# A hybrid encoder layer on one core: the first job tile by tile, dummy products meanwhile, x one tile further ahead, the last weights in other buffers

## The chip, the cores and the metric

The kernel runs on one core of a Trainium2 chip. The metric is the device time of one execution in microseconds; with several executions the median counts.

## The reference

One layer is applied to a prompt of 2048 tokens and to 8 samples of 16 tokens, with the same weights. A normed input is multiplied by one wide matrix; its columns feed a short convolution, a gated recurrence and a stick-breaking attention, and three gates merge them.

```python
def mixer_layer(x, l, conv_past, S0, past_k, past_v, norm_g, w_in, conv_w, lb, ...):
    h = rms_norm(x, norm_g[l])
    (a_x, a_b, a_c, a_z, g_q, g_f, g_i, g_z,
     s_q, s_k, s_v, s_z, m_a, m_b, m_c) = split_cols(h @ w_in[l])      # 1024 x 9216
    y_conv, conv_new = causal_conv(a_c * a_x, conv_w[l], conv_past)
    o_a = a_b * y_conv * jax.nn.silu(a_z)
    ...                                                                # f = lb + (1-lb) sigmoid(g_f), k = 1 - f
    S_new, o_hg = hgrn_scan(S0, q_hg, log_f, k_in, v_hg)
    o_b = rms_norm(o_hg, hg_norm_g[l]).reshape(B, T, W_HG) * jax.nn.silu(g_z)
    q = rms_norm(s_q, q_norm_g[l]); k = rms_norm(s_k, k_norm_g[l]); v = s_v
    o_sb = sb_prompt(q, k, v)                                          # or, for samples, over 1024 cached keys
    o_c = o_sb.reshape(B, T, W_SB) * jax.nn.silu(s_z)
    m = (jax.nn.sigmoid(m_a) * (o_a @ wb_a) + jax.nn.sigmoid(m_b) * (o_b @ wb_b)
         + jax.nn.sigmoid(m_c) * (o_c @ wb_c))
    return x + m @ w_out[l], conv_new, S_new, k, v
```

## The kernel before

TensorE (PE) does every product in float32 by splitting both operands into a high and a low part and adding three products (high-high, high-low, low-high). `split` makes the parts: ScalarE (ACT) copies to the high part (L174), VectorE (DVE) subtracts it to get the low part (L175). GpSimd (POOL) computes the powers of the norms (`rstd_of`, L211 and L213) and fills masks. All DMAs are issued by SyncE (SP), in one queue.

**Tokens.** There are 17 tiles of 128 tokens: tile 0 holds the samples, the others the prompt. They form three groups, each of two chunks: tiles 0-2 and 3-4, then 5-7 and 8-10, then 11-13 and 14-16. `Prepare` readies a group. For a tile, it loads x into `xt` (L562), squares and sums it on ACT (L569), takes the root on POOL, scales it by the root and by `g_bc`, the norm's gain in all partitions, on DVE (L574), transposes it on PE in two halves of four blocks (L585), and splits each half into `hh` and `hl`. In groups 2 and 3 two tiles are loaded at first, since the pool of `xt` has two buffers, and tile i + 2 is loaded once tile i is transposed. In group 1 all five tiles are loaded at the start, and the first chunk, three tiles, is made ready before the first job.

**Jobs.** For a group, `run_jobs` goes through the columns of `w_in` in jobs. A channel job holds 128 columns still on PE and moves up to 384 tokens of a chunk (`proj_chan`, L660: 24 products for each chunk). A token job (keys `sk`, values `sv`, queries `sq`, recurrence values `gi`) holds the tokens still and moves 256 columns (`proj_tok`, L671: 24 products for each tile). The accumulators (`acc`) are two buffers in this phase. `wload` loads a job's weights in pieces of 512 KB into `wst`, two buffers, and splits them into `w`, three buffers; `wkeep` stores the split weights, 1 MB each, as `W...`, from which later groups load them (L190). Group 1 begins with the gate columns `sz` as a channel job, and the second job is `sk`; job 0 and job 1 run on the first chunk, then both on the second.

**Between and after.** Generators run beside the jobs by a credit of time: the recurrence (`hbg`), attention of the samples during group 2, attention of the prompt from the end of group 2 on (`bg`). `open_attention` opens the pool `at` for the latter; its loads are Q (L260, L261), K (L266) and V (L270). Then follows the merge: for four groups of tiles, jobs multiply the branches by `w_branch` (L1328) and four jobs by `w_out` (L1363), the latter in two weight pieces each. `oh` and `ol` hold the split branch outputs there, two buffers each; a row block `xr` of x is added to an accumulator (L1371) and stored from `yt`. The four output jobs of the last group end the program.

The order in which an engine gets its instructions is set by the framework's scheduler from the order in the program and the buffers; `tc.issue_after(i)` only puts instructions behind `i` on its engine's queue.

## Time and profile before

| | |
|---|---|
| three runs | 2935.62, 2947.18, 2946.2 us; median 2946.2 |
| the profiled execution's own time | 2939.97 us |
| its span | 2938.3 us |
| mean granted clock of TensorE | 0.997 |

In the rows of the profile, times are in microseconds from the span's start unless marked ns. A row of the order of time gives start, length, engine, line, operation, output and inputs with shapes, count, and in brackets how long the engine stood idle before it and who released it. A row of a stretch gives its length and, for PE, weight loads (PEld), DVE, ACT and POOL in turn, busy time and instructions, then the granted clock, the share of DMA and GB/s. `SPq` is SP issuing. A bare piece like `0.44 PE tp L585 x4` comes from the chain of work that ended last, in order of time.

### The profile page before, as it was taken

To read this page: it belongs to the slowest core of one execution; us is meant where nothing else is said; L and a number is where in the kernel's file an instruction comes from. 1 tells how busy PE (TensorE), PEld (TensorE's weight loads), DVE (VectorE), ACT (ScalarE), POOL (GpSimd) and SP (SyncE) were. 2 spreads that over 40 slices of the span, in tenths; PEclk is the share of its full clock that TensorE was granted. 3 is DMA by queue.
4 is the path that set the end of the run, shared out by engine and by line. 5 is a ranking of instruction groups with operands and counts; after the bars stand their busy time and mean duration, and the time that the engine had idled before them with its cause. 6 is when DMAs were issued, how large, how long until landed. Compare 5 with 4: busy or idle time off the path is not lost.

```text
span 2938.3 us, 51261 instructions
## 1 busy us (share of the span) xinstructions
PE 2877.3 (98%) x19467; PEld 2672.8 (91%) x19467; DVE 1533.2 (52%) x3182; ACT 1024.5 (35%) x2359; POOL 429.4 (15%) x859
## 2 busy tenths in 40 slices
PE   8999999999999999999999999999999999999998
PEld 7999999989999999999999999999988787687888
DVE  5345635641342423345434748265677876767743
ACT  4332222242222222114333344334444554444420
POOL 3100000120100000003231111101013412313110
PEclk9999999999999999999999999999999999999999
DMA  8887776767556564535764443434347776677666
GB/s 280 302 272 237 229 229 231 233 224 244 183 192 198 175 211 146 177 128 170 243 193 156 139 153 129 163 116 153 125 148 265 253 263 215 224 234 232 233 229 211
DMA packets 329223, 597.80 MB, mean 203 GB/s; under 512 B 29097, under 2 KB 231170, under 8 KB 291090
## 3 DMA queue, kind: packets, MB, share of 16 engines
q1 hardware_dynamic: 328978, 594.54, 61.5%
q8 instruction: 154, 2.52, 0.4%
q14 instruction: 91, 0.75, 0.1%
HBM read 410.62 MB, written 183.80 MB: 202 GB/s over the span
## 4 chain that ended last, share of the span: by engine, by line
PE 87%; DMA 4%; DVE 3%; issue 3%; POOL 1%; ACT 1%; SPq 0%; DVEq 0%; POOLq 0%; ACTq 0%
PE acc L660 44%; PE acc L671 13%; PE acc L1363 6%; PE acc L1328 5%; PE pv L334 4%; PE tp L289 3%; PE z L985 2%; PE z L305 2%; PE z L304 2%; DMA w<-W 2%; DVE pr L317 1%; PE tp L432 1%; POOL mp L1337 1%; PE pv L496 1%; DMA ost<-OX 1%
## 5 line engine op out<-in xcount | busy, mean ns | idle before, releaser
L660 PE MATMUL acc<-hh,w 128*128 128x384 f32 (+1 forms) x5376 | 1466.5, 338 | 1.3 <-ACT w L174 0.8
L660 PEld LDWEIGHTS acc<-hh,w 128*128 128x128 f32 x5376 | 965.6, 188 | 25.6 <-issue 17.9
L660 PE MATMUL acc<-hl,w 128*128 128x384 f32 (+1 forms) x2688 | 883.3, 329 | 0.0
L660 PEld LDWEIGHTS acc<-hl,w 128*128 128x128 f32 x2688 | 507.9, 189 | 4.9 <-issue 1.0
L671 PE MATMUL acc<-w,hh 128*128 128x256 f32 x2176 | 411.6, 285 | 0.7 <-DVE gm L1078 0.4
L671 PEld LDWEIGHTS acc<-w,hh 128*128 128x128 f32 x2176 | 341.6, 188 | 2.7 <-DVE gm L1078 0.7
L317 DVE TENSOR_TENSOR_SCAN pr<-snb,carry 128x513 f32<-128x513 f32 x192 | 250.8, 1307 | 118.3 <-ACT snb L308 116.8
L671 PE MATMUL acc<-w,hl 128*128 128x256 f32 x1088 | 306.4, 282 | 0.0
L1328 PE MATMUL acc<-oh,w 128*128 128x512 f32 (+2 forms) x960 | 296.6, 370 | 4.0 <-ACT oh L174 2.5
L290 ACT COPY aT<-tp 128x512 f32<-128x512 f32 (+2 forms) x320 | 167.4, 524 | 290.9 <-PE tp L289 290.6
L322 DVE TENSOR_TENSOR sp<-sp,pr 128x512 f32<-128x512 f32 (+2 forms) x320 | 210.2, 657 | 34.7 <-POOL sp L313 10.0
L1363 PE MATMUL acc<-w,mh 128*128 128x256 f32 x1088 | 212.8, 285 | 7.6 <-DMA w<-W 7.5
L308 ACT ACTIVATE snb<-z 128x512 f32<-128x512 f32 (+2 forms) x320 | 172.3, 539 | 127.9 <-PE z L305 117.2
L1328 PEld LDWEIGHTS acc<-oh,w 128*128 128x128 f32 x960 | 177.5, 191 | 36.4 <-DVE gate L1336 4.4
L671 PEld LDWEIGHTS acc<-w,hl 128*128 128x128 f32 x1088 | 205.2, 189 | 0.4
L317 DVE TENSOR_TENSOR_SCAN pr<-snb,one 128x129 f32<-128x129 f32 (+3 forms) x128 | 115.7, 904 | 160.1 <-POOL snb L313 159.8
L1363 PEld LDWEIGHTS acc<-w,mh 128*128 128x128 f32 x1088 | 173.6, 188 | 17.1 <-issue 6.7
L175 DVE TENSOR_TENSOR w<-wst,w 128x1024 fp32r<-128x1024 f32 x92 | 114.9, 1249 | 137.1 <-ACT w L174 134.7
L289 PE MATMUL tp<-idf,sp 128*128 128x128 f32 x1088 | 172.8, 274 | 8.3 <-ACT aT L290 7.7
L1328 PE MATMUL acc<-ol,w 128*128 128x512 f32 (+1 forms) x480 | 174.7, 364 | 2.7 <-DVE ol L175 2.6
L310 ACT ACTIVATE sp<-z 128x512 f32<-128x512 f32 (+2 forms) x320 | 171.4, 536 | 11.9 <-DMA OX<-ot 6.7
L289 PEld LDWEIGHTS tp<-idf,sp 128*128 128x128 f32 x1088 | 132.0, 141 | 27.3 <-ACT aT L290 10.1
(290 smaller groups left out, 3620.5 us busy)
## 6 DMA issues: line engine op xcount, KB each, us to landing
w<-W SPq DMA_DIRECT2D x204, 1024.0 KB, 5.4
W<-w SPq DMA_DIRECT2D x92, 1024.0 KB, 5.0
wst<-in_w_in_dram SPq DMA_DIRECT2D x72, 512.0 KB, 5.5
GM<-gm SPq DMA_DIRECT2D x120, 192.0 KB, 2.8
Kt<-KT SPq DMA_DIRECT2D x160, 128.0 KB, 3.6
gate<-GM SPq DMA_DIRECT2D x72, 256.0 KB, 3.0
vc<-in_cache_v_dram SPq DMA_DIRECT2D x64, 256.0 KB, 3.2
kc<-in_cache_k_dram SPq DMA_DIRECT2D x64, 256.0 KB, 2.9
```

Source lines behind the costliest of these rows:

```text
L175: return first, (eng or nc.vector).tensor_tensor(lo, src, hi.bitcast(F32), ALU.subtract)
L289: nc.tensor.transpose(tp[:, j * P:(j + 1) * P], sp[:, j * P:(j + 1) * P], idf)
L290: nc.scalar.copy(aT[:, e, 0:nb, i * P:(i + 1) * P], tp[:, :w].rearrange("p (b q) -> p b q", q=P))
L308: nc.scalar.activation(sn[:, 512 - w:512], z[:, :w], AF.Sigmoid, scale=-0.125)
L310: nc.scalar.activation(sp[:, :w], z[:, :w], AF.Sigmoid, scale=0.125)
L317: nc.vector.tensor_tensor_scan(pr[:, 512 - w:513][:, ::-1], s_in, s_in, one if diag else carry[e][i], ALU.mult, ALU.bypass)
L322: nc.vector.tensor_tensor(sp[:, :w], sp[:, :w], pr[:, 513 - w:513], ALU.mult)
L334: nc.tensor.matmul(pv[64 * e:64 * e + 64, c0:n], Vt[:, j, e], aT[:, e, j, c0:n], start=first and j == 0, stop=last and j == nb - 1, skip_g ...
L660: nc.tensor.matmul(acc[:, :n], w[0][a][:, k], hT[b][:, k, :n], start=k == 0 and i == 0, stop=k == KB - 1 and i == 2)
L671: nc.tensor.matmul(acc[:, :256], hT[b][:, k, ti * P:(ti + 1) * P], w[k // 4][a][:, k % 4], start=k == 0 and i == 0, stop=k == KB - 1 and i ...
L1328: nc.tensor.matmul(acc[:, :n], w[0][a][:, k, dd * P:(dd + 1) * P], box[x][b][:, k, sl], start=k == 0 and i == 0, stop=k == 3 and i == 2)
L1363: nc.tensor.matmul(acc[:, :256], box["l" if b else "h"][:, k, ti * P:(ti + 1) * P], w[k // 4][a][:, k % 4], start=k == 0 and i == 0, stop= ...
```

## The change

1. Group 1 starts with the first job on V (`sv`, columns 0 to 255), and this job runs on both chunks before the next. It asks for one tile at a time (`Prepare.tile`), so a tile's square, scaling and transposes stand between the products of the tile before. x of tile 0 and `g_bc` are loaded first, then the job's two weight pieces, then the other four tiles.
2. `keep_busy` puts products of the identity with itself on PE, whose result nobody reads: 14 at the start, four behind each half of tile 0's transposes.
3. The vectors, masks, fills and `rev` are built behind the first job's preparation instead of ahead of or beside it.
4. A third buffer for x (pool `xq`): groups 2 and 3 load three tiles at first and tile i + 3 once tile i is transposed (in group 3 the last tiles go to the two old buffers). The pool is closed before attention's opens, and the first chunk of group 3 is made ready ahead of that.
5. The weights of the last group's second and fourth output job go into buffers of `oh` and `ol`.

```diff
-    first_split = []
-    def wload(pieces, key):
+    def wload(pieces, key, places=None):
...
-            w = wp.tile([P, 2, 1024], F32R, tag="w", name="w")
+            w = places[n] if places else wp.tile([P, 2, 1024], F32R, tag="w", name="w")
...
                 st = wp.tile([P, a, b], F32, tag="wst", name="wst", bufs=2)
                 nc.sync.dma_start(st, v)
-                pair = split(hi, lo, st)
-                if not first_split:
-                    first_split.extend(pair)
+                with ExitStack() as order:
+                    if len(kept) < 1 and n:
+                        for x in prep.last:
+                            order.enter_context(tc.issue_after(x.ins))
+                    split(hi, lo, st)
...
+    p01 = ExitStack()
+    xq = p01.enter_context(tc.tile_pool(name="xq", bufs=1, side="right"))
...
+    def keep_busy(n):
+        z = ps_z()
+        for _ in range(n):
+            nc.tensor.matmul(z[:, 0:P], idf, idf, start=True, stop=True)
+    keep_busy(14)
...
+            self.final = g == len(GROUPS) - 1
...
         def load(self, i):
-            self.fetch(i, xp.tile([P, D], F32, tag="xt", name="xt"))
+            self.fetch(i, self.room(i))
             self.square(i)
+        def room(self, i):
+            return (xq.tile([P, D], F32, tag="xt3", name="xt3") if i == 2 or i % 3 == 2 and not self.final else
+                    xp.tile([P, D], F32, tag="xt", name="xt"))
...
-                for i in range(min(2, n)):
+                for i in range(min(3, n)):
...
-                if i + 2 < n:
-                    self.load(i + 2)
-                    yield
-                if i + 1 >= 2 and i + 1 < n:
-                    self.scale(i + 1)
+                for k in [i + 2] if self.final and i == 3 else [] if self.final and i == 2 else [i + 3]:
+                    if k < n:
+                        self.load(k)
+                        yield
+                if i + 2 >= 3 and i + 2 < n:
+                    self.scale(i + 2)
                     yield
                 self.ready = i
...
-            for i in range(n):
-                self.fetch(i, xp.tile([P, D], F32, tag="xt", name="xt") if i < 2 else
-                           g0p.tile([P, D], F32, tag="xt0", name="xt0", bufs=3))
-                if i == 0:
-                    nc.sync.dma_start(g_bc, norm_g[0].partition_broadcast(P))
-            for f in (self.square, self.scale):
-                for i in range(2):
-                    f(i)
             self.scaled = True
             for i in range(n):
-                if i > 2:
-                    with tc.issue_after(first_split[0].ins), tc.issue_after(first_split[1].ins):
-                        self.square(i)
-                        yield
-                        self.scale(i)
-                        yield
+                if not i:
+                    self.fetch(i, self.room(i))
+                    nc.sync.dma_start(g_bc, norm_g[0].partition_broadcast(P))
+                with ExitStack() as order:
+                    if i:
+                        for x in self.last:
+                            order.enter_context(tc.issue_after(x.ins))
+                    for k in ((0,), (1, 2), (3,), (4,), ())[i]:
+                        self.square(k)
+                    yield
+                    self.scale(i)
+                yield
                 for kk in range(0, KB, 4):
                     self.turn(i, kk)
+                    if not i:
+                        keep_busy(4)
                     yield
-                    if i == 0 and not kk:
-                        self.square(2)
-                if i == 0:
-                    with tc.issue_after(self.last[1].ins):
-                        self.scale(2)
                 self.ready = i
-                yield
+                if not i:
+                    yield
+                    for k in range(1, n):
+                        self.fetch(k, self.room(k) if k < 3 else g0p.tile([P, D], F32, tag="xt0", name="xt0", bufs=2))
...
+            return self.hT[ci]
+        def tile(self, ci, ti):
+            i = self.tiles.index((ci, ti, self.group[ci][ti]))
+            while self.ready < i:
+                next(self.gen)
             return self.hT[ci]
...
-    prep.chunk(0)
+    prep.tile(0, 0)
...
+    def build_vectors():
+        nc.sync.dma_start(qg_bc, q_norm_g[0].partition_broadcast(P))
+        nc.sync.dma_start(kg_bc, k_norm_g[0].partition_broadcast(P))
+        vrow = g0p.tile([17, P], F32, tag="mtmp", name="vrow", bufs=2)
+        nc.sync.dma_start(vrow[0:12], conv_w[0].rearrange("j (b p) -> (j b) p", p=P))
+        nc.sync.dma_start(vrow[12:16], hg_lb_logits[0].rearrange("(h p) -> h p", p=P))
+        nc.sync.dma_start(vrow[16:17], hg_norm_g)
+        pvec = ps_tp()
+        nc.tensor.transpose(pvec[:, 0:17], vrow, idf[0:17, 0:17])
+        nc.vector.tensor_copy(vec, pvec[:, 0:17])
...
+                    acc = yield from proj_tok(w, hT(ti) if callable(hT) else hT, ti)
         filler = [sz_job(j) for j in range(4)] + [gate_job(x, d) for x in range(3) for d in range(8)]
+        if not g:
+            jobs.append(qkv.pop(2))
...
-        order = ([(0, 0), (1, 0), (0, 1), (1, 1)] + order
+        begin = [(0, 0), (1, 0), (0, 1), (1, 1)] if g else [(0, 0), (0, 1), (1, 0), (1, 1)]
+        order = (begin + order
                  + [(n - 2, 0), (n - 1, 0), (n - 2, 1), (n - 1, 1)])
         for at_, (i, ci) in enumerate(order):
             weights(i)
-            weights(i + 1)
-            if not g and at_ == 1:
-                with tc.issue_after(rstd_at[0].ins), tc.issue_after(first_split[1].ins):
+            if g or at_:
+                weights(i + 1)
+            if not g and at_ == 0:
+                prep.advance()
+            if not g and at_ == 2:
+                with tc.issue_after(rstd_at[0].ins), tc.issue_after(prep.last[1].ins):
+                    build_vectors()
+                    build_hist()
+                    build_rev()
                     build_bound()
                     build_masks()
                     build_selectors()
-            hT = prep.chunk(ci)
+            hT = prep.chunk(ci) if g or at_ > 1 else lambda ti, ci=ci: prep.tile(ci, ti)
...
-                if nxt and (left <= 2 or nxt.ready < 0 and len(nxt.xt) < 2 or left <= 3 and not nxt.scaled):
+                if nxt and (left <= 2 or nxt.ready < 0 and len(nxt.xt) < 3 or left <= 3 and not nxt.scaled):
...
+            prep.chunk(0)
             bg.drain()
+            p01.close()
             open_attention()
...
-            ws[i + 1] = wload(*alljobs[i + 1][0])
+            places = None
+            if i + 1 - len(alljobs) in (-3, -1):
+                places = [p3.tile([P, 4, GMAX], F32R, tag=t, name="wlast", bufs=2).rearrange("p a b -> p (a b)")
+                          [:, :2048].rearrange("p (v w) -> p v w", v=2) for t in ("oh", "ol")]
+            ws[i + 1] = wload(*alljobs[i + 1][0], places)
```

`build_hist` (the fills of `uhist`, `shist`, `cstage` and the load of the cached convolution rows) and `build_rev` hold lines that stood at the top level before, as `build_vectors` does. What the scheduler makes of this stands below, engine by engine, at the places where instructions move.

PE, the first instructions; before, x of three tiles is transposed, then the first channel job starts (`vrow` holds the vectors):

```order
L585 MATMUL tp<-idf,xt 128x128 x16
L585 MATMUL tp<-idf,xt_117 128x128 x8
L704 MATMUL tp<-idf,vrow 128x17
L660 MATMUL acc<-hh,w 128x384
L660 MATMUL acc<-hl,w 128x384
L660 MATMUL acc<-hh,w 128x384 x2
```

and now (L553 is `keep_busy`, L602 the transposes, L694 the token job):

```order
L553 MATMUL z<-idf 128x128 x14
L602 MATMUL tp<-idf,xt 128x128 x4
L553 MATMUL z<-idf 128x128 x4
L602 MATMUL tp<-idf,xt 128x128 x4
L553 MATMUL z<-idf 128x128 x4
L694 MATMUL acc<-w,hh 128x256
L694 MATMUL acc<-w,hl 128x256
```

The products of tile 0 follow its own transposes, with 22 dummies around those.

DVE, behind its first five instructions; before:

```order
L574 SCALAR_TENSOR_TENSOR xt<-xt,rr,g_bc 128x1024 x2
L175 TENSOR_TENSOR hl<-tp,hh 128x4x128 x2
L574 SCALAR_TENSOR_TENSOR xt_117<-xt_117,rr,g_bc 128x1024
L175 TENSOR_TENSOR hl<-tp,hh 128x4x128 x4
L706 COPY vec<-tp 128x17
L175 TENSOR_TENSOR w<-wst,w 128x1024
```

and now:

```order
L591 SCALAR_TENSOR_TENSOR xt<-xt,rr,g_bc 128x1024
L175 TENSOR_TENSOR w<-wst,w 128x1024
L175 TENSOR_TENSOR hl<-tp,hh 128x4x128 x2
L175 TENSOR_TENSOR w<-wst,w 128x1024
L591 SCALAR_TENSOR_TENSOR xt<-xt,rr,g_bc 128x1024
L175 TENSOR_TENSOR hl<-tp,hh 128x4x128 x2
```

The remainders of the two weight pieces now stand between the first tile's steps, and a tile's scaling stands behind the low parts of the tile before; the masks, the vectors and the bound follow after the fifth tile, ahead of the first gate product.

SP, the first loads for the prompt's attention; before, at the end of the samples' attention (L528 is its last store):

```order
L528 DMA OX<-oct 128x4x128
L889 DMA OX<-y 128x384
L260 DMA Q_15008<-QT 64x512
L261 DMA Q_15009<-QT 64x512
L190 DMA w<-W_5548 128x2048
```

and now, at the end of group 2 (L579 loads x, L262 and L263 Q, L268 K, L272 V):

```order
L579 DMA xt<-in_x_prompt_dram 128x1024
L1092 DMA OX<-ob 128x256
L1147 DMA GM<-gm 128x384
L262 DMA Q_15038<-QT 64x512
L263 DMA Q_15039<-QT 64x512
L579 DMA xt<-in_x_prompt_dram 128x1024
L262 DMA Q_15038<-QT 64x512
L263 DMA Q_15039<-QT 64x512
L268 DMA Kt<-KT 64x512 x2
L272 DMA Vt<-VV 128x4x128
```

The first heads' Q, K and V moved behind the late loads of group 3's x, one of which stands among them.

SP, the weights of the last jobs, before (L1320 loads a gate, L1358 `xr`; the last two pairs are W_27241, W_27243 and W_27586, W_27588):

```order
L190 DMA w<-W_26519 128x2048
L1320 DMA gate<-GM 128x512 x2
L190 DMA w<-W_26521 128x2048
L1320 DMA gate<-GM 128x512
L190 DMA w<-W_26872 128x2048
L1372 DMA out_dram<-yt 128x256
```

and now (`wlast` is a buffer of `oh` or `ol`; the pairs' numbers are 29 higher):

```order
L189 DMA w<-W_26548 128x2048
L1360 DMA gate<-GM 128x512
L189 DMA w<-W_26550 128x2048
L1360 DMA gate<-GM 128x512 x2
L189 DMA wlast<-W_26901 128x2048
L189 DMA w<-W_27270 128x2048
L189 DMA wlast<-W_27615 128x2048
L1412 DMA out_dram<-yt 128x256 x2
```

The second pair, of which W_26903 went out earlier still, and the first pieces of the third and fourth are now ahead of the first store of the last output rows.

More of the change, by code (lines that the diff above doesn't have):

```diff
@@ L689, in trunk @@
     prep = Prepare(0)
-    prep.chunk(0)
+    prep.tile(0, 0)
     qg_bc = const.tile([P, 64], F32, name="qg_bc")
-    nc.sync.dma_start(qg_bc, q_norm_g[0].partition_broadcast(P))
     kg_bc = const.tile([P, 64], F32, name="kg_bc")
-    nc.sync.dma_start(kg_bc, k_norm_g[0].partition_broadcast(P))
-    vrow = g0p.tile([17, P], F32, tag="mtmp", name="vrow", bufs=2)
-    nc.sync.dma_start(vrow[0:12], conv_w[0].rearrange("j (b p) -> (j b) p", p=P))
-    nc.sync.dma_start(vrow[12:16], hg_lb_logits[0].rearrange("(h p) -> h p", p=P))
-    nc.sync.dma_start(vrow[16:17], hg_norm_g)
-    pvec = ps_tp()
-    nc.tensor.transpose(pvec[:, 0:17], vrow, idf[0:17, 0:17])
-    vec = const.tile([P, 17], F32, name="vec")
-    nc.vector.tensor_copy(vec, pvec[:, 0:17])
+    vec = const.tile([P, 17], F32, name="vec")
+    def build_vectors():
[8 more added lines that the diff above has]
+        nc.vector.tensor_copy(vec, pvec[:, 0:17])
     def tap(j, b):
@@ L1087, in compute @@
                 for ti, t in enumerate(chunks[ci]):
-                    acc = yield from proj_tok(w, hT, ti)
+                    acc = yield from proj_tok(w, hT(ti) if callable(hT) else hT, ti)
                     post(acc, t, s)
```

16 lines of the change are left out of this document (9 added, 7 removed).

## The prediction

> **What bounds the kernel now.** I read the page's first part, then the busy time in stretches chosen around PE's idle time, then the order of time in the stretches that the change touches.
>
> ```profile
> span 2938.3 us, 51261 instructions
> ...
> PE 2877.3 (98%) x19467; PEld 2672.8 (91%) x19467; DVE 1533.2 (52%) x3182; ACT 1024.5 (35%) x2359; POOL 429.4 (15%) x859
> ...
> 0.00:32.24 32.24, 19.72 (x91) 17.61 (x92) 18.45 (x39) 17.03 (x26) 15.12 (x62) 1.00 0.81 270
> ...
> 570.00:612.00 42.00, 37.34 (x259) 34.25 (x257) 23.91 (x59) 16.63 (x41) 7.09 (x14) 1.00 0.77 261
> ...
> 1340.00:1365.00 25.00, 20.69 (x128) 18.95 (x127) 18.39 (x28) 14.20 (x34) 9.15 (x18) 1.00 0.64 216
> ...
> 2196.00:2880.00 684.00, 655.88 (x3910) 539.99 (x3910) 481.55 (x612) 301.31 (x589) 172.81 (x265) 0.99 0.72 238
> 2880.00:2938.30 58.30, 50.39 (x398) 48.30 (x396) 13.45 (x26) 2.30 (x4) 0.00 (x0) 1.00 0.60 202
> ```
>
> TensorE (PE) is busy 2877.3 of 2938.3 us, so every saving is PE idle time or PE time at a low clock. The second number of a stretch row is PE's busy time. Idle: 12.5 us in the first stretch, 4.7 and 4.3 where one token group follows another, 28.1 in the merge stage, 7.9 at the end: 57.5 of all 61.0. The change works on all of these but the merge stage; in the order of instructions nothing is changed from 1365 us to the last output jobs, so the 28.1 us stay.
>
> The start is worse than its 12.5 idle us, as PE also runs slowly there:
>
> ```profile
> 1.18 0.29 POOL masks.py:199 TENSOR_SCALAR_AFFINE_SELECT idf<-idf 128x128 f32<-128x128 f32 x1
> 4.62 1.06 ACT L569 ACTIVATE junk<-xt 128x1024 bf16<-128x1024 f32 x1 [2.55 <-DMA xt<-in_x_sample_dram]
> 6.98 1.29 DVE L574 SCALAR_TENSOR_TENSOR xt<-xt,rr,g_bc 128x1024 f32<-128x1024 f32 x1 [5.24 <-POOL rr L213]
> 7.83 1.06 ACT L569 ACTIVATE junk<-xt 128x1024 bf16<-128x1024 f32 x1 [2.06 <-DMA xt<-in_x_prompt_dram]
> 8.32 1.97 PE L585 MATMUL tp<-idf,xt 128*128 128x128 f32 x8 [8.32 <-DVE xt L574]
> 9.80 0.57 POOL L213 TENSOR_TENSOR rr<-rv,mhalf 128x1 f32<-128x1 f32 x1
> 13.50 0.59 ACT L174 CAST hh<-tp 128x512 fp32r<-128x512 f32 x1 [2.28 <-PE tp L585]
> 14.12 0.69 DVE L175 TENSOR_TENSOR hl<-tp,hh 128x512 fp32r<-128x512 f32 x1
> 17.36 1.05 ACT L174 CAST w<-wst 128x1024 fp32r<-128x1024 f32 x1
> 18.44 1.23 DVE L175 TENSOR_TENSOR w<-wst,w 128x1024 fp32r<-128x1024 f32 x1 [0.17 <-ACT w L174]
> 18.46 0.69 PE L660 MATMUL acc<-hh,w 128*128 128x384 f32 x1 [0.78 <-ACT w L174]
> ...
> 21.80 0.84 PE L660 MATMUL acc<-hh,w 128*128 128x384 f32 x2
> ...
> 24.64 0.59 PE L660 MATMUL acc<-hh,w 128*128 128x384 f32 x1
> ...
> 28.67 0.44 PE tp L585 x4
> ...
> 97.93 7.07 PE acc L660 x48
> 105.00 14.24 PE acc L671 x120
> ```
>
> The last three rows are pieces of the chain: warm, a transpose takes 0.11 us (0.44/4), a 256-column product 0.119 (14.24/120), and a 384-column one 0.178 (7.07 for 24 of each). Cold, eight transposes took 1.97 us, 0.246 each. The first projection starts at 18.46 and the pace stays cold to 24.64. Up to 32.24 us PE did 40 transposes and 48 products of 384 columns, the work of 4.4 + 8.5 = 12.9 warm us: 19.3 us are lost there.
>
> **The start.** The first job is now V's projection (24 products of 256 columns per tile), taken tile by tile as x arrives, its two weight pieces second and third in the queue after g_bc; 14 dummy products stand in front, four more behind each half of the first tile's transposes. Up to the first x tile the chain is the old one: x lands at 4.6, is scaled from 6.98, transposes at 8.32. The dummies can start at 1.5, when the identity is written. An f32 product with 128 columns shows as two records:
>
> ```profile
> 594.52 0.39 PE L1030 MATMUL hg<-vg,sc 128*128 128x128 f32 x2
> 594.74 0.40 PE L1032 MATMUL hg<-Sn,Qd 128*128 128x128 f32 x2
> ...
> 2337.61 0.66 PE L289 MATMUL tp<-idf,sp 128*128 128x128 f32 x4 [2.11 <-ACT aT L290]
> ...
> 2702.35 1.12 PE L289 MATMUL tp<-idf,sp 128*128 128x128 f32 x4 [3.28 <-ACT aT L290]
> ```
>
> The first two rows start 0.22 us apart, so a warm dummy costs 0.22, a cold one 0.49 by the transposes' ratio. Fourteen cold ones take 6.9 us and end at 8.4. PE worked 6.2 us, from 18.46 to 24.64, until it was warm; from 1.5 that is 7.7, so 25 cold records and 3 warm ones end at 8.0. PE stays warm until 8.32: a gap of 2.11 us before 2337.61 left it warm (four transposes in 0.66), while one of 3.28 before 2702.35 did not (1.12). [...]
>
> First tile: transposes 8.32, two batches of four dummies of 0.88 each between and behind, PE free at 11.1. The landings: x0 was there at 4.6 and x1, two DMAs on, at 7.8, so 1.6 us each; a 512 KB weight piece takes 1.95 at the first stretch's mean of 270 GB/s. So w0, where x1 stood, lands near 8.2, w1 near 10.1, x1 near 11.7. ACT: w0's copy (1.05) from 8.2, both halves of hh (0.59) to 10.9, w1's copy to 11.95, then x1's square (1.06 and its read). DVE: w0's remainder (1.23) to 10.5, two hl (0.69) to 11.9, w1's remainder to 13.2. First product at 11.2, tile done at 14.4. x1's square ends at 13.2, POOL's two steps take 0.9, scaling 1.28 from 14.15; transposes at 15.45, product at 17.35. From then a tile needs on DVE and its partners 1.28 + 0.55 (four transposes and latency) + 0.59 + 2 x 0.69 + 0.1 = 3.9 us, on PE 2.85 + 0.88 = 3.73. Three more tiles at 3.9, the last late by about 0.6 for the next weights' remainder on DVE: the job ends at 17.35 + 3 x 3.9 + 0.6 + 2.85 = 32.5. PE has then done 120 products and 40 transposes, 18.7 warm us; before it had 13.2 at that time (12.9 at 32.24 and 0.26 on). **Gain 5.5 us.** Bounds: 7.0 if PE sets the period from the second tile; 2.0 if weights land at half x's pace and the dummies stay cold. The 22 dummies cost nothing else: PE has nothing to do there.
>
> The constants (masks, bound, vectors) moved behind this job stand in DVE's queue ahead of the first gate product, whose accumulator the third accumulator after it needs.
>
> ```profile
> 23.18 0.29 POOL L740 MEMSET mtmp<- 128x128 f32 x2
> ...
> 30.97 0.32 POOL L745 TENSOR_SCALAR_AFFINE_SELECT mtmp<-mtmp 128x1 f32<-128x1 f32 x2
> ```
>
> Before, POOL's masks took 8.1 us between these rows, other fills among them. Now DVE is free for the first at 30.5, by the schedule above; 8.1 us more put the gate product at 38.6, and PE needs the buffer at 32.5 + 7.1 = 39.6. Hidden by 1 us; slower masks would cost what they exceed that by. Stores of V wait on SP for ACT's copies with weight loads behind them, needed 14 us later: nothing.
>
> **x three tiles ahead.** In both later groups the third tile now has a buffer of its own, so each late load comes one tile sooner.
>
> ```profile
> 593.59 1.09 PE L585 MATMUL tp<-idf,xt 128*128 128x128 f32 x8 [0.89 <-DVE xt L574]
> ...
> 605.18 0.65 PE L585 MATMUL tp<-idf,xt 128*128 128x128 f32 x4 [0.49 <-DVE hl L175]
> ...
> 1343.38 0.44 PE L1058 MATMUL tp<-idf,on 128*128 128x128 f32 x2 [0.97 <-DVE hl L175]
> ...
> 1355.98 0.66 PE L585 MATMUL tp<-idf,xt 128*128 128x128 f32 x4 [1.70 <-DVE hl L175]
> ...
> 1362.08 1.06 PE L585 MATMUL tp<-idf,xt 128*128 128x128 f32 x8 [1.15 <-DVE xt L574]
> ```
>
> Waits on x or on what follows it: 0.89 + 0.49 = 1.4 us in the first transition, 0.97 + 1.70 + 1.15 = 3.8 in the second. A tile sooner is about 6 us there (the last two tiles' transposes stand at 1355.98 and 1362.08), more than each wait. But recurrence and attention steps are re-sorted there, and what comes late next is DVE. I take **1.0** (0 to 1.4, and a loss of 1 if the recurrence waits instead) and **2.8** (0 to 3.8). Against the second stands that attention's Q and K loads no longer come early (first rival).
>
> **Last weights.** Output jobs two and four of the last group load into the free oh/ol buffers, so no load waits for the running job.
>
> ```profile
> 2885.76 0.36 PE L1363 MATMUL acc<-w,mh 128*128 128x256 f32 x1 [0.69 <-DMA w<-W]
> ...
> 2899.98 0.39 PE L1363 MATMUL acc<-w,mh 128*128 128x256 f32 x1 [0.28 <-DMA w<-W]
> ...
> 2913.32 0.39 PE L1363 MATMUL acc<-w,mh 128*128 128x256 f32 x1 [1.44 <-DMA w<-W]
> ...
> 2927.04 0.38 PE L1363 MATMUL acc<-w,mh 128*128 128x256 f32 x1 [1.94 <-DMA w<-W]
> ```
>
> The waits are 0.69 + 0.28 + 1.44 + 1.94 = 4.35 us. The last three go (3.66); of the first, whose load now comes one gate load sooner, I take half: **4.0**. Bytes are the same. Next late are xr and y stores, but three accumulators at 2.85 us per tile cover them.
>
> **Sum:** 5.5 + 1.0 + 2.8 + 4.0 = 13.3 off an execution of 2939.97 us (span 2938.3): 2926.7. That execution lies 6.2 below the median of the three runs, 2946.2; against the median, 2946.2 - 13.3 = 2932.9, say 2933, 0.45% less. About 0.5% (14.7 us, 2931.5) is what a measurement of this kernel can tell from no change.
>
> **Rivals.**
> (1) Slower: the new pool must close before attention's pool opens, so the first Q, K, V loads, issued near 1190 us before, now come after the third tile's transposes, with an x load among them that waits for a buffer:
>
> ```profile
> 1190.47 0.52 SPq L260 DMA_DIRECT2D Q<-QT  x1
> ...
> Kt<-KT SPq DMA_DIRECT2D x160, 128.0 KB, 3.6
> ```
>
> Two heads' loads are 13 issues of 0.5 us and a landing of 3.6, with the wait for the x buffer 12.8 us. In the new order PE has 19 transposes and some 41 products, 9.4 us, before the first score, which needs only the first half (8.9). If all 12.8 were uncovered and PE cold after (2.6 more), 15.4 is lost and the 2.8 too: 2946.2 - 10.5 + 15.4 = 2951. It decides once more than 10.5 is uncovered; the cover of 9.4 speaks against.
> (2) The front pays less: the dummies do not release the clock and hold the transposes (8.32 to 14.3 for both batches, about 2.5 us), and each tile takes 4.4 on DVE (1.5 more). Start 1.5: 2937.
> (3) All waits vanish and PE sets the first job's period: 7.0 + 1.4 + 3.8 + 4.35 = 16.6: 2929.6.
> (4) The x loads change nothing, since DVE was the wait: 2946.2 - 9.5 = 2936.7.
>
> **Chances.** Forecast 0.50, (1) 0.04, (2) 0.15, (3) 0.25, (4) 0.06. The runs shown spread from 2935.62 to 2947.18, so the forecast's own range is 2927 to 2938, of which a third is beyond 0.5%: faster 0.25 x 0.85 + 0.5 x 0.36 = 0.39; slower 0.02, part of (1); within 0.59. Range 2922 to 2943: the bounds summed are gains of 16.6 and 4.6 (2.0 - 1 + 0 + 3.6), 2929.6 and 2941.6; the runs' spread adds to both sides, more to the fast one, where the shown times reach 10.6 below their median.
>
> **What would show it.** Dummies from 1.5 to about 8; the first tile's transposes warm; L694 from about 11.4; first job done near 32.5, then no PE gap before 60; PE idle in the first 32 us near 9 with the dummies counted as busy; waits on x gone at both transitions; no wait for w at the end. Wrong if the first products start after 14, if a PE wait for Q or K stands at the second transition, or if the gate product holds PE near 39.

## The result, and the profile after

| | before | after |
|---|---|---|
| first comparison, median | 2946.2 us (5 runs, 2935.62 to 2947.2) | 2922.81 us (5 runs, 2919.97 to 2925.84) |
| ratio, 95% interval | | 0.9932 [0.9919, 0.9945] |
| second and third comparison, ratio | | 0.9949 [0.9936, 0.9962], 0.9942 [0.9930, 0.9954] |
| all executions, median | 2938.95 us (78 runs) | 2922.94 us (15 runs) |
| profiled execution: span, own time, clock | 2938.3, 2939.97, 0.997 | 2918.1, 2919.97, 0.999 |

The change is faster, by 23.4 us in the first medians, by 20.2 us between the two profiled spans, and by 16.0 us between the medians of all executions. The forecast was 13.3 us: 2933 against the first median, 2926.7 against the profiled execution; the range of 2922 to 2943 held the time at its fast end. The three shown times of before had a high median: 78 executions give one 7.3 us lower. So of the 10.1 us by which 2933 was too slow, 7.3 are the median that it started from.

The profile after, first its totals, then the busy time of the first stretch (its granted clock reads 1.00, as before's did, since the column holds 1.00 until the first recorded change, at 25.01 us in before and 4.43 in after; the cold start shows only in the paces of the rows below):

```profile
span 2918.1 us, 51343 instructions
...
PE 2873.3 (98%) x19511; PEld 2672.2 (92%) x19511; DVE 1530.7 (52%) x3182; ACT 1024.7 (35%) x2359; POOL 427.9 (15%) x859
```

```profile
0.00:32.24 32.24, 27.14 (x202) 25.27 (x203) 17.00 (x26) 17.28 (x29) 12.60 (x36) 1.00 0.90 315
```

PE's idle time is 44.8 us instead of 61.0, in the first 32.24 us 5.1 instead of 12.5. The start in order of time:

```profile
1.46 4.80 PE L553 MATMUL z<-idf 128*128 128x128 f32 x28 [1.46 <-POOL idf masks.py:199]
8.17 0.66 PE L602 MATMUL tp<-idf,xt 128*128 128x128 f32 x4 [1.91 <-DVE xt L591]
8.66 1.06 PE L553 MATMUL z<-idf 128*128 128x128 f32 x8
9.55 0.60 PE L602 MATMUL tp<-idf,xt 128*128 128x128 f32 x4
9.99 1.06 PE L553 MATMUL z<-idf 128*128 128x128 f32 x8
10.80 0.36 PE L694 MATMUL acc<-w,hh 128*128 128x256 f32 x1
...
15.16 1.07 PE L602 MATMUL tp<-idf,xt 128*128 128x128 f32 x8 [0.67 <-DVE xt L591]
...
39.02 0.55 DVE L1106 TENSOR_TENSOR gm<-acc,gm 128x384 f32<-128x384 f32 x1
```

The dummies warm PE (28 records in 4.80 us, 0.21 us apart at first and 0.11 from 4.4 us on), the transposes run warm (four in 0.66 us), the first product starts at 10.80 and the second tile's transposes at 15.16. Up to 32.24 us PE did 40 transposes, 117 products of 256 columns and one of 384, or 4.4 + 13.9 + 0.2 = 18.5 warm us: 13.7 are lost instead of 19.3. The first gate product on DVE (L1106) starts at 39.02 and PE waits for nothing there. The transitions, PE's rows with a wait of 0.3 us or more:

```profile
589.15 0.44 PE L1086 MATMUL tp<-idf,on 128*128 128x128 f32 x2 [1.82 <-DVE hl L175]
599.09 0.66 PE L434 MATMUL tp<-idf,kc 128*128 128x128 f32 x4 [0.63 <-DVE hl L175]
616.81 0.39 PE L694 MATMUL acc<-w,hh 128*128 128x256 f32 x1 [1.19 <-DMA w<-W]
...
1334.21 0.44 PE L1086 MATMUL tp<-idf,on 128*128 128x128 f32 x2 [0.97 <-DVE hl L175]
1342.25 0.63 PE L602 MATMUL tp<-idf,xt 128*128 128x128 f32 x4 [0.40 <-DVE xt L591]
1348.22 0.52 PE L602 MATMUL tp<-idf,xt 128*128 128x128 f32 x3 [1.38 <-DVE xt L591]
1351.90 0.33 PE L291 MATMUL tp<-idf,sp 128*128 128x128 f32 x1 [0.46 <-DVE hl L175]
```

In the first, no transpose of x waits any more; in the second, the waits are 0.97, 0.40, 1.38 and 0.46 where they were 0.97, 1.70 and 1.15. The last piece of PE in the chain that ended last:

```profile
2870.90 44.04 PE acc L1403 x366
```

There is no wait for weights in the output jobs. Set against the same instructions of the profiled execution of before, the 20.2 us come from: the start 5.7, the first transition 3.0, the second 0.9, the merge stage (before: 2193 to 2844 us) 5.0, the end behind it 5.2, all else 0.4. (Where the start ends, one channel job of 7.07 us stands on the other side of the recurrence's steps; it is taken out here.)

### The profile page after: what moved, and what is told of

Read it like the earlier page. It is cut to its first block, busy times and chain, and to the rows that moved or that the text cites. A ratio compares the mean times of both kernels' runs of the same rounds, so it can differ in the third digit from the quotient of the medians.

```text
span 2918.1 us, 51343 instructions
## 1 busy us (share of the span) xinstructions
PE 2873.3 (98%) x19511; PEld 2672.2 (92%) x19511; DVE 1530.7 (52%) x3182; ACT 1024.7 (35%) x2359; POOL 427.9 (15%) x859
## 4 chain that ended last, share of the span: by engine, by line
PE 87%; DVE 4%; DMA 4%; issue 3%; POOL 2%; ACT 1%; SPq 0%; DVEq 0%; POOLq 0%; ACTq 0%
PE acc L683 45%; PE acc L694 13%; PE acc L1403 6%; PE acc L1368 4%; PE pv L336 4%; PE tp L291 3%; PE z L1013 2%; PE z L307 2%; PE z L306 2%; DVE pr L319 1%; PE tp L434 1%; POOL mp L1377 1%; DMA w<-W 1%; PE pv L498 1%; DMA gate<-GM 1%
## 5 line engine op out<-in xcount | busy, mean ns | idle before, releaser
L694 PE MATMUL acc<-w,hh 128*128 128x256 f32 x2176 | 413.1, 286 | 1.5 <-DMA w<-W 1.2
L694 PEld LDWEIGHTS acc<-w,hh 128*128 128x128 f32 x2176 | 341.8, 188 | 4.0 <-DMA w<-W 1.5
L694 PE MATMUL acc<-w,hl 128*128 128x256 f32 x1088 | 306.8, 282 | 0.7 <-DVE hl L175 0.7
L694 PEld LDWEIGHTS acc<-w,hl 128*128 128x128 f32 x1088 | 205.1, 189 | 1.8 <-DVE hl L175 1.3
L1403 PE MATMUL acc<-w,mh 128*128 128x256 f32 x960 | 189.1, 285 | 2.5 <-DMA w<-W 2.3
L1403 PEld LDWEIGHTS acc<-w,mh 128*128 128x128 f32 x960 | 153.7, 188 | 10.6 <-issue 5.2
L1146 ACT ACTIVATE gm<-acc 128x384 f32<-128x384 f32 (+1 forms) x144 | 68.3, 474 | 260.8 <-PE acc L683 223.0
```

The lines of the kernel that those rows point to most:

```text
L694: nc.tensor.matmul(acc[:, :256], hT[b][:, k, ti * P:(ti + 1) * P], w[k // 4][a][:, k % 4], start=k == 0 and i == 0, stop=k == KB - 1 and i ...
L1403: nc.tensor.matmul(acc[:, :256], box["l" if b else "h"][:, k, ti * P:(ti + 1) * P], w[k // 4][a][:, k % 4], start=k == 0 and i == 0, stop= ...
```

## The experiments

"Start", "transition", "merge" and "end" are differences to the profiled execution of before, between the same instructions, in us; positive is faster.

| run | kernel | ratio to before, 95% interval | start | 1st transition | 2nd | merge | end |
|---|---|---|---|---|---|---|---|
| e1 | before again | 1.0005 [0.9995, 1.0015] | -2.3 | 0.0 | 0.8 | -2.7 | 1.2 |
| e2 | start alone | 0.9979 [0.9970, 0.9989] | 5.5 | -2.6 | 1.0 | 1.8 | 1.5 |
| e3 | x alone | 0.9989 [0.9978, 0.9999] | -0.8 | 1.8 | 0.6 | -3.6 | 1.6 |
| e4 | last weights alone | 0.9984 [0.9975, 0.9993] | 0.6 | 0.3 | 0.8 | 2.5 | 1.8 |
| e5 | after again | 0.9949 [0.9936, 0.9962] | 5.8 | 2.1 | 0.5 | 1.9 | 4.3 |
| e6 | after, x two ahead | 0.9957 [0.9945, 0.9968] | 5.8 | -1.3 | 0.5 | 2.3 | 4.0 |
| e7 | after, no dummies | 0.9963 [0.9949, 0.9976] | 3.7 | 3.9 | 1.2 | 4.4 | 4.7 |
| e8 | after, 7 dummies at first | none: one execution, 2929.2 us | 3.2 | 2.4 | -0.6 | 0.8 | 4.5 |
| e9 | after, last weights in order | 0.9952 [0.9939, 0.9964] | 5.5 | 3.4 | 0.0 | 3.0 | 6.0 |
| e10 | e9, no dummies | 0.9970 [0.9960, 0.9980] | 3.1 | 4.3 | 0.3 | -1.1 | 6.2 |
| e11 | after, third time | 0.9942 [0.9930, 0.9954] | 5.6 | 4.5 | 0.2 | 5.0 | 4.1 |

The places that a run's kernel leaves as they were (all of e1's) show what executions of one program differ by: up to 2 or 3 us in a place.

**e1, the kernel before again** (no edit).

> The kernel before, unchanged, to get a second trace and the clock beside each time. From 1365 us to the last jobs both traces hold the same instructions, yet the changed kernel was 4.8 us shorter there (2193 to 2878 us before). Theory A: this is not the change's, but the number of cold spells of TensorE after its long waits, which differs from execution to execution; then the runs here spread over 6 us or more, the longer ones have the lower mean clock (0.995 against 0.998), and the stage's idle time stays within 1.5 us of 28.1. Theory B: the stage is shorter because of the change (other times of its loads); then this trace is within 1 us of the first there, and the spread does not go with the clock.

Its profiled execution took 2943.66 us, with PE at a mean clock of 0.996, and it lost 2.7 us in the merge stage against the first. (A cold spell is a time in which PE is granted half its clock, in before for one 0.50 from 2291.46 to 2294.87 us.) Stretches of 20 us of the merge stage with a clock under 1.00, first of before, then of before again, then of after:

```profile
2280.00:2300.00 20.00, 16.40 (x93) 13.86 (x92) 18.75 (x20) 10.45 (x19) 8.20 (x9) 0.91 0.86 275
2300.00:2320.00 20.00, 19.91 (x110) 16.68 (x111) 18.28 (x26) 9.88 (x20) 10.60 (x8) 0.91 0.66 227
2560.00:2580.00 20.00, 18.95 (x106) 13.90 (x107) 13.18 (x18) 8.49 (x17) 0.00 (x0) 0.91 0.72 230
2700.00:2720.00 20.00, 17.65 (x75) 12.66 (x76) 12.04 (x18) 8.45 (x20) 9.71 (x17) 0.83 0.69 222
```

```profile
2200.00:2220.00 20.00, 17.89 (x93) 13.27 (x92) 14.76 (x20) 11.50 (x21) 0.00 (x0) 0.91 0.61 199
2280.00:2300.00 20.00, 16.87 (x99) 14.45 (x96) 17.40 (x19) 9.17 (x16) 8.67 (x9) 0.91 0.78 257
2300.00:2320.00 20.00, 18.22 (x106) 15.82 (x106) 19.29 (x27) 10.53 (x21) 8.37 (x9) 0.91 0.68 235
2340.00:2360.00 20.00, 17.89 (x93) 13.45 (x92) 14.90 (x24) 10.41 (x25) 9.05 (x17) 0.91 0.77 259
2560.00:2580.00 20.00, 17.72 (x104) 12.42 (x103) 11.38 (x17) 8.20 (x16) 0.00 (x0) 0.91 0.67 209
2700.00:2720.00 20.00, 16.96 (x80) 11.95 (x79) 12.19 (x18) 8.19 (x19) 9.81 (x16) 0.91 0.71 210
2760.00:2780.00 20.00, 17.61 (x93) 12.99 (x92) 14.39 (x18) 5.91 (x11) 1.26 (x7) 0.91 0.74 260
```

```profile
2280.00:2300.00 20.00, 18.44 (x109) 16.89 (x110) 19.66 (x24) 11.15 (x21) 8.45 (x9) 0.91 0.76 250
2680.00:2700.00 20.00, 16.75 (x78) 11.64 (x77) 13.13 (x18) 7.09 (x16) 10.16 (x16) 0.91 0.74 233
```

A clock of 0.91 over 20 us is 1.8 us less, or 3.6 at half the clock. Summed over stretches of 10 us, the clock lost in the merge stage was, in all 13 traces, a whole number of times 1.7 us (3.4 at half):

| trace | times 1.7 us | stage's length | its idle time |
|---|---|---|---|
| after | 2 | 646.0 | 27.0 |
| e11 | 3 | 646.1 | 26.2 |
| e2, e4, e5, e7 | 4 | 649.2, 648.5, 649.2, 646.7 | 28.0, 25.8, 27.1, 25.7 |
| before, e8, e9, e10 | 5 | 651.0, 650.2, 648.0, 652.1 | 28.1, 27.0, 25.2, 28.6 |
| e6 | 6 | 648.7 | 25.8 |
| e1, e3 | 7 | 653.7, 654.6 | 27.8, 28.9 |

The length goes with the clock lost, 0.94 us for each (correlation 0.84), while the idle time hardly changes. Over the 73 executions of before whose clock is known, the mean time falls from 2945.6 us at a clock of 0.994 (3 runs) to 2939.0 at 0.997 (34) and 2934.6 at 0.999 (4). What theory A named is there: the 5.0 us that the merge stage gave between the two profiled executions are three cold spells fewer, and executions of one program differ by as many (before again lost 2.7 there with two more; the changed kernel has 2, 4 and 3 in after, e5 and e11). Whether the change makes the spells a little rarer isn't settled: the four traces with all of its parts have 2, 3, 4 and 5, those without any 5 and 7, and the mean granted clock is 0.9976 over the 15 executions of the changed kernel and 0.9970 over the 73, which would be 1.8 us (an estimate, 0.0006 of 2940).

**e2 to e4, each part alone.** Start alone is the changed kernel without the lines on `xq`, on three tiles and on `wlast`; x alone and last weights alone are the kernel before with these lines:

```diff
# x alone
+    xq = p01.enter_context(tc.tile_pool(name="xq", bufs=1, side="right"))
-            self.fetch(i, xp.tile([P, D], F32, tag="xt", name="xt"))
+            self.fetch(i, self.room(i))
-                for i in range(min(2, n)):
+                for i in range(min(3, n)):
...
# last weights alone
+            if i + 1 - len(alljobs) in (-3, -1):
+                places = [p3.tile(...) for t in ("oh", "ol")]
```

> Of the change only the start: the first job on V tile by tile, the dummies, the later constants; x two tiles ahead as before, the last weights in their old buffers. Theory A (the parts add up, each at its own place): 19.3 us lost to the first job's end fall to 13.7, a gain of 5.7 us (ratio 0.998), both transitions and the tail as before: waits on x near 1.4 and 3.8 us, four waits for w of 4.35 at the end. Theory B (the start shifts later loads and thus shortens the merge stage): 10 us or more, ratio 0.9965.

> Of the change only the third buffer for x in groups 2 and 3. Theory A: TensorE idles 2.5 us less in the first transition (570 to 612 us) and about 1 less in the second, of which a late weight load behind the first gives back 0.9: a gain of 2.7 us, ratio 0.999. Theory B (the x loads bring the merge stage's 4.8 too, since attention's first loads moved): 7.5 us, ratio 0.9975. Theory C (the waits there are DVE's, so the loads change nothing): 0.5 us or less.

> Of the change only the buffers of the second and fourth output job's weights. Theory A: the last 55 us become 5.2 us shorter (4.4 idle, 0.8 of restarts), no wait for w there, all else as before: ratio 0.9982. Theory B (the merge stage's 4.8 come from these buffers too, through the order of the loads): 10 us, ratio 0.9966. If only the waits themselves go, without restarts: 4.35.

The ratios are 0.9979, 0.9989 and 0.9984: theory A in all three, 6.2 + 3.2 + 4.7 = 14.1 us. (x alone has an interval of 0.3 to 6.5 us.) The traces add two things. Start alone: 19.3 us lost became 13.7, but the first transition became 2.6 us longer, which theory A did not expect:

```profile
597.48 1.06 ACT L583 ACTIVATE junk<-xt 128x1024 bf16<-128x1024 f32 x1 [1.99 <-DMA xt<-in_x_prompt_dram]
```

```profile
590.61 0.63 PE L599 MATMUL tp<-idf,xt 128*128 128x128 f32 x4 [1.96 <-DVE xt L588]
607.29 1.26 PE L599 MATMUL tp<-idf,xt 128*128 128x128 f32 x8 [1.92 <-DVE xt L588]
```

```profile
580.00:600.00 20.00, 17.76 (x121) 16.96 (x120) 8.29 (x13) 9.53 (x23) 3.11 (x8) 0.91 0.60 222
```

ACT waits for an x tile to land, PE waits twice for what follows, and a cold spell comes on top. With the first job moved, the recurrence's steps stand one channel job (48 products, 7.07 us) earlier against the jobs. Last weights alone: the four waits of the output jobs are gone, but a new one stands ahead of them, with PE cold behind it (two products in 1.05 us instead of 0.62):

```profile
2869.99 0.76 PE L1328 MATMUL acc<-oh,w 128*128 128x512 f32 x1 [2.54 <-DMA w<-W]
```

SP's rows for it, last weights alone, then the same loads before:

```profile
2855.66 1.57 SPq L1320 DMA_DIRECT2D gate<-GM  x2
2857.32 0.38 SPq L190 DMA_DIRECT2D wlast<-W  x1
2862.07 0.32 SPq L1320 DMA_DIRECT2D gate<-GM  x1
2862.48 0.38 SPq L190 DMA_DIRECT2D w<-W  x1
```

```profile
2859.21 1.57 SPq L1320 DMA_DIRECT2D gate<-GM  x2
2860.88 0.38 SPq L190 DMA_DIRECT2D w<-W  x1
```

The program there is 4.5 us ahead of before. The branch weights, issued right behind two gate loads before, now stand behind `wlast` and one more gate load, which waits until DVE has used its buffer: they go out 1.6 us later by the clock, 6.1 later against the program.

**e5 and e6, the changed kernel with and without x three tiles ahead.** e6 takes the lines on `xq` and three tiles back out.

> The changed kernel once more, beside the next three. The three parts alone gave ratios of 0.9979, 0.9989 and 0.9984, 6.2 + 3.2 + 4.7 = 14.1 us. Theory A (the parts only add): 0.9952, a median near 2924 beside 2938. Theory B (x three tiles ahead is worth more once the first job is moved, since the start alone raised the waits on x in the first transition to 1.96 + 1.92 us and made TensorE cold there): 0.9935, near 2919.

> The changed kernel with x two tiles ahead as before. Theory A (parts add): 3 us slower than the changed kernel, ratio to the kernel before 0.9963. Theory B (interaction): waits on x of 1.9 us twice in the first transition and a stretch there at a clock of 0.91, together 5 to 6 us slower than the changed kernel, again 0.996; the difference between this and the changed kernel decides.

The changed kernel came at 0.9949, e6 at 0.9957, medians 2925.97 and 2928.55. In these two times theory A (the parts add) fits best; over the three comparisons of the changed kernel the gains are 20.0, 15.0 and 17.0 us, 17.4 on average, between the 14.1 of theory A and the 19 of theory B, so the times leave it open. Theory B's mechanism is in the traces, but its size is not in the ratio: x ahead is worth 1.8 us at the first transition with the old start, and about 5 with the new one (2.1, 4.5, 3.4 and 3.0 with it, -1.3 and -2.6 without), of which the times, 0.8 of a thousandth apart with intervals of 1.2, can't tell more. In the second transition it is worth nothing: -0.6 to 1.2 in eight traces with it, 0.5 to 1.0 in four without.

**e7, e8 and e10, the dummies.** e7 takes out all 22, e8 has 7 at the start in place of 14:

```diff
-    keep_busy(14)
+    keep_busy(7)
```

> The changed kernel without its 22 dummy products. Theory A (they warm the clock): the eight transposes of the first tile take 1.97 us instead of 1.2, a product of 256 columns 0.24 instead of 0.12 for the first 3 to 6 us of work, the second tile's transposes start 2 to 3 us later than 15.2, and the first job ends 2 to 3 us later than 32.4. Theory B (VectorE sets the pace of that job): the cold products run beside VectorE's chain, and the end moves by under 0.7 us.

> The changed kernel with 7 instead of 14 dummies at the start: 14 records of 0.21 us from 1.5, so they end near 4.6 and TensorE stands idle 3.5 us until its first transposes near 8.2. In the changed kernel the record's pace changed from 0.21 to 0.11 after 12 or 13 of them, 2.9 us after the first, and an idle time of 1.91 us left it warm. Theory A (clock is released after about 2.9 us of work and lost in a wait of over 3 us): the transposes start cold, four in about 1.0 us instead of 0.66. Theory B (it is lost only after longer waits): four in 0.66.

The start without dummies, then with 7:

```profile
7.96 1.97 PE L601 MATMUL tp<-idf,xt 128*128 128x128 f32 x8 [7.96 <-DVE xt L590]
9.85 0.58 PE L691 MATMUL acc<-w,hh 128*128 128x256 f32 x1
11.22 0.58 PE L691 MATMUL acc<-w,hl 128*128 128x256 f32 x1 [0.79 <-DVE hl L175]
```

```profile
1.46 3.35 PE L553 MATMUL z<-idf 128*128 128x128 f32 x14 [1.46 <-POOL idf masks.py:199]
8.03 0.66 PE L602 MATMUL tp<-idf,xt 128*128 128x128 f32 x4 [3.22 <-DVE xt L591]
8.52 1.66 PE L553 MATMUL z<-idf 128*128 128x128 f32 x8
9.98 1.06 PE L602 MATMUL tp<-idf,xt 128*128 128x128 f32 x4
10.83 1.72 PE L553 MATMUL z<-idf 128*128 128x128 f32 x8
12.30 0.36 PE L694 MATMUL acc<-w,hh 128*128 128x256 f32 x1
```

Without dummies PE is cold until 14.6 us in e7 and 16.3 in e10 (two products of 256 columns in 0.63 us, behind that in 0.40), and yet the first job ends only 0.6 and 1.6 us later than in the changed kernel (0.6 of e10's since its first transposes start at 8.59 instead of 7.96): the cold products run beside the second tile's chain on ACT and DVE, which is theory B in e7. With 7, neither theory: the first four transposes behind the 3.22 us of waiting are warm (0.66 us), and the clock falls right behind them, at 8.8, for 3.4 us (e8's stretches up to there and from there on; PE was busy for 0.77 us of the first):

```profile
5.39:8.80 3.41, 0.77 (x7) 0.77 (x8) 1.28 (x1) 0.96 (x3) 0.75 (x2) 1.00 1.06 356
8.81:12.21 3.40, 3.40 (x18) 3.40 (x18) 2.34 (x3) 2.03 (x4) 0.00 (x0) 0.50 1.03 410
```

The dummies behind the transposes then take 1.66 and 1.72 us for eight records instead of 1.06 and delay the first product to 12.30, later than with none at all.

> The same without the 22 dummies, to see again what they are worth. In the trace without them the first job ended 0.6 us later, but five further times lay 4 us above those of the changed kernel. Theory A (0.6 us is all, the rest was spread): the ratio to e9's kernel is 1.0002, and in the trace the first job ends 0.6 us later. Theory B (they bring more): 3 to 4 us slower than with them, and a place in the trace other than the first job shows it.

The times lie 4 to 7 us above those with dummies (18 executions without, median 2929.6; 15 of the changed kernel, 2922.9), so theory B's size, and a place for part of it: between the first job and 560 us another 1.1 to 1.4 us are lost, among them waits like this one of e7, which no trace with 14 dummies has:

```profile
143.06 0.39 PE L691 MATMUL acc<-w,hh 128*128 128x256 f32 x1 [1.06 <-ACT kn L785]
```

The dummies also stand in the scheduler's reckoning: without them ACT, DVE, POOL and SP get some of their instructions of the first jobs in another order. That this order brings the wait is not shown: e1 and e3 wait there for `kn` too, 0.70 and 0.55 us, and before and e4, with the same start, do not. The first job and this stretch make the 2.0 to 2.5 us by which the column "start" falls. The remaining 2 to 4 us of the difference are not placed. Some may be cold spells: the mean granted clock of the 18 executions is 0.9968 beside 0.9976 with the dummies, about 2.3 us (an estimate, 0.0008 of 2925). In e10's trace a late weight load is part of it, for which PE waits 2.74 us from 784.91 on, with a cold spell behind (two products in 0.63 us); e7 doesn't have it.

**e9, the last weights in order.**

```diff
+                    if places:
+                        behind.enter_context(tc.issue_after(last_w[-1].ins))
+                    last_w.append(nc.sync.dma_start(w.bitcast(F32), kept[key, n].bitcast(F32)))
```

> The changed kernel with the second output job's two weight loads into oh and ol issued behind the weights of the jobs ahead of them. In the changed kernel the load into ol goes out earlier, so a gate load that waits for its buffer gets in front of the last but one branch weights, and TensorE waits for those: 2.54, 1.83, 0.98, 0.80, 0.61 and 0.20 us in six traces, in the longest one with TensorE cold behind it. Theory A (that order is the cause): the wait for branch weights between 2855 and 2875 us is gone as in the traces of before, none of the four waits of the output jobs returns but the first (0.5 to 0.7 us), and the end of the program is 0.5 to 1 us sooner against the changed kernel's average. Theory B (the weights are late for another reason, the bandwidth): the wait stays at 0.6 to 1.8 us.

No wait for branch weights stands between 2855 us and the end in e9 or e10, while e11, beside them, has one of 1.40. (e10 has one of 1.18 ahead of that stretch, at 2841.32, where e1 and e3, without the new buffers, wait 1.00 and 0.59 too.) In e9 the end's last piece is one run of all 384 products:

```profile
2870.88 45.94 PE acc L1407 x384
```

Theory A holds in the trace, and brings more than the 0.5 to 1 us expected: the column "end" is 6.0 and 6.2 against 4.1 on average in the seven traces with `wlast` in the old order. It is 2 us of 2920, and the ratio (0.9952 against 0.9942 for e11) can't show it: a version better than the changed kernel by its trace, not by its time.

> The changed kernel a third time, beside the two versions above. If the parts only add up: 13 to 15 us under the kernel before (0.9949 to 0.9955); if the first comparison's ratio of 0.9932 is the typical one: 20 us.

0.9942 is 17.0 us; with the other two comparisons and e1's spread, the first one's 0.9932 is at the lucky end.

## Why the prediction came out as it did

**The start: right, for a reason that was half right.** 5.5 us were forecast, 5.7 came (5.5 to 5.8 in five further traces; the old start itself differs by -2.3 to 0.6 in e1, e3 and e4). The first product was put at 11.2 (10.80), the second tile's transposes at 15.45 (15.16), the job's end at 32.5 (32.7). The dummies' end was put at 8.0; it was 6.26, since PE became warm 2.9 us after their start in this trace, and 3.2 to 4.8 us in five others, not after 6.2. Rival (2), dummies that leave PE cold and hold the transposes, did not come; nearest to it is e8, where the later eight dummies are cold and hold the first product. PE's idle time in the first 32 us was put near 9 and was 5.1: of the 13.7 us lost, the dummies are 6.9. (The 9 does not follow from the prediction's own steps, which leave 32.5 - 18.7 - 8.3 = 5.5 beside the dummies, nor does the bound of 7.0, which comes out as 6.6.) The constants were hidden: gate product on DVE at 39.0 (forecast 38.6), no wait on PE.

**First transition: the term was too small.** 1.0 was forecast from the waits of before (0.89 + 0.49), 3.2 is the mean of four traces. The step that failed took those waits as they stood, while the new start raises them: start alone lost 2.6 us here. The bound of 1.4 was therefore no bound. Nor is all of the 3.2 shown to be x's: a wait of 1.51 us for the recurrence (`hg<-Sn,Qd`, at 571.76 in before), which the term did not count, stands in e1, e3 and e4 too (1.50 to 1.73) and is gone in the four traces. A late weight load (1.19 in after, 1.52 in e5, none in e11) gave part back.

**Second transition: the term was wrong.** 2.8 was forecast, 0.4 is the mean of the four traces with the whole change, and 0.6 that of five without x ahead, before among them. The step said that a tile sooner, 6 us, is more than each wait. The last x load did go sooner, at 1339.77 instead of 1351.96, but PE's transposes of that tile moved forward in its queue with it, to 1348.22 from 1362.08, and the last tile, which still waits for an old buffer, is again what PE waits for (the load before, then after):

```profile
1351.96 0.33 SPq L562 DMA_DIRECT2D xt<-in_x_prompt_dram  x1
```

```profile
1339.77 0.34 SPq L579 DMA_DIRECT2D xt<-in_x_prompt_dram  x1
```

```profile
1344.70 1.06 ACT L586 ACTIVATE junk<-xt 128x1024 bf16<-128x1024 f32 x1 [0.58 <-DMA xt<-in_x_prompt_dram]
```

From its landing, the square, POOL's steps and the scaling lead to the transposes at 1348.22 and their wait of 1.38. Rival (1) did not come: PE waits nowhere there for Q or K, and the waits are 3.2 us in all; the 2.6 us that this rival puts on a cold PE are shown by no run.

**Last weights: the waits went, and a new one came.** All four waits are gone (forecast: three and a half of them, 4.0). The profiled execution of before had the longest end of those without the change, by 1.2 to 1.6 us, so against their average the change brings about 3.0. The step that failed is "what is late next": I named xr and the stores of y, and it was the branch weights ahead of the output jobs, behind `wlast` and a gate load on SP. The order of before and after showed it; I read there that a load comes one gate load sooner and didn't follow the queue further back.

**The merge stage: forecast 0, and 0 but for its spells.** Its idle time stayed (28.1 before, 27.0 after), and what it gave between the two profiled executions is cold spells. The prediction took these spreads for the runs' and widened the fast end for them, which is why the range held 2922.81, by 0.8 us. The chances leaned the other way: 0.59 for a change within 0.5% and 0.39 for one beyond it, where the three ratios are 0.68%, 0.51% and 0.58%.

So the sum of 13.3 stands against 16.0 between the medians of all executions. It came out near by luck in part, since the first transition's error (+2.2) and the second's (-2.4) cancel. The terms as measured make 5.7 + 3.2 + 0.4 + 3.0 = 12.3, and the 4 to 5 us up to the 16.0 and the 17.4 of the three comparisons stay open; rarer cold spells in the merge stage, where the four traces are 3.7 us shorter on average than the profiled execution of before and e1 is 2.7 longer, could be most of it, but two traces without the change can't show that. Of its rivals, (3), "everything vanishes" with 16.6, is nearest in size but not in its terms, and (4) is right for the second transition alone.

## What to carry to other kernels

Trace a moved load back through its whole queue: a load that gets its buffer earlier is issued earlier, and takes other loads' places (with `wlast` ahead of them the branch weights went out 6.1 us later against the program); put it behind them by hand when they are needed first. A wait of before is no bound for what a change there can bring, when another part of the change moves the work that covers it. In the merge stage, where TensorE stands idle for 1 to 3 us at a time (3.28 before 2702.35), executions differed by whole cold spells, 2 to 7 in the 13 traces: compare such a stage by idle time and lost clock, not by length.

## What the runs showed of the hardware

- Cold spells came in whole steps: 1.7 us of clock lost, 3.4 us at half the clock (in before a granted clock of 0.50 from 2291.46 to 2294.87 us), 2 to 7 of them in the same 650 us of the 13 traces, and the stage's length, which spread over 8.6 us, went with them (correlation 0.84).
- In the traces of before and after all recorded changes of the clock lie whole multiples of 3.413 us apart, wherever the waits are (in before from 25.01 to 2939.99 us, 854 such steps). Counted back to the start of the span, the first step begins at 1.12 us in before, at 1.02 in after, and, from the fall at 8.81, at 1.98 in e8. Of the steps at full clock in before and after, from the first recorded change on, all 3 in which PE was busy for less than 44% (1.22 and 1.42 us in before, 0.61 in after) were followed by one at half clock, none of the 1679 with more than 60%, and 3 of the 17 between. So in these two traces whether a wait of 1 to 3 us cost 1.7 us of clock went with how much of it fell into one step; that this makes the spread of the merge stage is argued from it and not tested by a run.
- PE became warm 2.9, 3.2, 3.3, 4.2, 4.2 and 4.8 us after the first dummy in six traces (after, e6, e5, e2, e11 and e9, whose first 28 records took 4.80, 4.87, 4.95, 5.35, 5.39 and 5.65 us).
- Waits shorter than 3.413 us ended warmth at times: 1.96 us did in e2, 1.91 did not in after, each in a step in which PE was busy for 54% (in after for 1.83 us of the step from 4.43). After 3.22 us (e8) the clock fell only 0.8 us after work had begun again, at the end of a step with 23%: there the dummies behind the transposes, cold themselves, delayed the work that they were to warm PE for, the first product to 12.30 from 10.80.
